# A two-layer hybrid token mixer: order of the transposed attention weights, and recurrence scores in half-width blocks

## The chip, the cores and the metric

The kernel runs on one core of one Trainium2 chip. The metric is the device time of one execution in microseconds; the time before is the median of three runs. TensorE (PE in the profile, its weight loads PEld), VectorE (DVE), ScalarE (ACT), GpSimd (POOL) and SyncE (SP, which issues most DMAs) each work through their own queue in program order and wait for each other by semaphores.

## The reference, cut to what matters

Two layers. Each one normalizes and modulates 512 latent and 256 context tokens of width 1024, mixes them, projects the result, and runs a SwiGLU. The mixer has three parts side by side; the change touches the first two.

```python
# recurrence: 4 heads of width 128, forward and reversed, in chunks
def step(state, inp):
    qi, ki, vi, gi = inp
    bcum = jnp.cumsum(gi, axis=2)
    o_inter = jnp.einsum('bhtk,bhkv->bhtv', qi * jnp.exp(bcum), state)
    rel = bcum[:, :, :, None, :] - bcum[:, :, None, :, :]
    decay = jnp.exp(jnp.where(incl, rel, -jnp.inf))
    scores = jnp.einsum('bhtk,bhsk,bhtsk->bhts', qi, ki, decay)
    o_intra = jnp.einsum('bhts,bhsv->bhtv', scores, vi)
    ...

# differential attention: 4 heads, two maps each
def diff_softmax_attend(q, keys, vals, lam):
    s = jnp.einsum('bqhmd,bkhmd->bhmqk', q, keys).astype(jnp.float32) * (DA_QK ** -0.5)
    p = jax.nn.softmax(s, axis=-1)
    w = p[:, :, 0] - lam * p[:, :, 1]
    return jnp.einsum('bhqk,bkhv->bqhv', w.astype(vals.dtype), vals)
```

Latent queries read 768 keys, context queries (layer 0 alone) the 256 context keys.

## The kernel before

All tokens stay on chip in one SBUF arena, cut into regions that the profile calls reg0 to reg8. PSUM is one tile P of eight banks of 512 columns. The large projections are split into a high and a low part and run as three fp32r matmuls (mm3); the recurrence and the attention's transposes and value products run in plain fp32.

The program is written by a planner. The class Builder holds a model of each engine's time (Clock). A main lane is a generator over the projections (mixer, wout, ffn); side lanes are generators for the recurrence (gla_levels, gla_post), the attention (attention) and others. A side lane yields the model time at which its next step can start; drive takes a main step, then the side steps that are due. So what stands between two steps of a side lane in TensorE's queue is the main lane's work, and the yielded times decide how much. A yield of free(b) is the model's time at which bank b has been read out; written(x) the time at which x is in place.

**Recurrence.** For each head gla_levels computes the scores of all chunks of 128 tokens (six in layer 0, four in layer 1) by seven levels. At level lev blocks of 2^lev tokens meet their neighbours: one matmul per chunk with KM as stationary operand and a strided view of QP as moving operand, into bank 3 or 4 and bank 5 (dst), then a predicated copy through a mask into the score tile. The mask of a level below 6 selects only pairs inside the same 64 tokens; level 6 selects the pairs across the two halves, and is already computed in two 64x64 matmuls per chunk, output partitions 0 to 63 and 64 to 127 in turn. One more group of matmuls, ahead of the loop, computes the diagonal's scores; ScalarE copies it whole. In the trace the levels are P<-reg2f,reg6f and, at level 6, P<-reg2f,reg3f in layer 0; P<-reg0f,reg8f and P<-reg0f,reg1f in layer 1. Each fp32 matmul is two rows.

**Attention.** One unit is a tile of 128 queries and a head: 24 units in layer 0 (16 with 768 keys, 8 with 256), 16 in layer 1. Iteration i of the loop works on four units at once: scores of unit i (two maps, each with a minimum on VectorE and an exponential on ScalarE), transposes of unit i-2 (six tiles, four into bank 4 and two into bank 5), weights of unit i-1 on VectorE, values of unit i-3. The value products vo(u) lie in the upper half of bank 5, so they cannot be written while an engine still reads the transposes in its lower half. transposed(u) copies the transposes out: all 768 columns by ScalarE, or 512 by ScalarE and 256 by VectorE (L280), as the model finds the engines less busy. In the trace the scores are P<-reg2r and P<-reg0r with 96 rows, the transposes P<-reg8f,reg3f and P<-reg8f,reg1f (L246), the values P<-reg6f,reg3f and P<-reg6f,reg1f with 64 columns, the minimum is L956.

Of the kernel before, what the change touches and what calls it, by code (L numbers as in the profile page):

```python
# [19 lines left out]
T = SEQ + CTX  # L20
# [130 lines left out]
class Builder:  # L151
# [580 lines left out]
    def gla_levels(self, h):  # L732
# [23 lines left out]
        def mixed(s):  # L756
            nb0 = (T - t0) // (2 * s)
            self.act(self.V(KM + t0, (2 * s, nb0), (s, 2), (1, s)), self.V(KS + t0, (2 * s, nb0), (s + T, 2), (1, s)))
        yield
        for c in chunks:  # L760
            self.mm(dst(1, c), self.S(self.osc(h, c), 128), self.S(q + c * 128, 128))
        for c, n, b, co in groups(1):
            self.act(self.S(self.osc(h, c), n * 128), self.B(b, n * 128, co))
        mixed(1)
# [2 lines left out]
        for lev in range(7):  # L767
            s = 1 << lev
            nb = T // (2 * s)
            dims = ((2 * s, 64 // s), (s + T, 2), (1, s))  # L770
            for c in chunks:
                if lev == 6:
                    for hf in range(2):
                        o = dst(lev, c, 64 * (1 - hf), 64)
                        self.mm(o[64 * hf:64 * hf + 64], self.S(KS + T * hf + 128 * c + 64 * hf, 64),
                                self.S(QP + T * (1 - hf) + 128 * c + 64 * (1 - hf), 64))
                else:
                    self.mm(dst(lev, c), self.S(KM + 128 * c, 128), self.V(QP + 128 * c, *dims))
            b0 = t0 // (2 * s)
            bd = ((2 * s, nb), (1, s))  # L780
            bl = ((2 * s, nb - b0), (1, s))
# [133 lines left out]
    def attention(self):  # L915
# [58 lines left out]
                self.stt(p0, p1, sm(u, 6), p0, ALU.mult, ALU.add)  # L974

        def transposes(u):
            for k in range(keys(units[u][1])[1]):
                self.tr(self.B(4, 128, k * 128), self.S(pr(u, 0) + k * 128, 128))

        def transposed(u):  # L980
            nk, _ = keys(units[u][1])
            wt = WT + (u % 2) * 768
            if nk < T or self.ck.t['ac'] < self.ck.t['dv']:
                self.act(self.S(wt, nk), self.W(2048, nk))
            else:
                self.act(self.S(wt, 512), self.B(4))
                self.copy(self.S(wt + 512, 256), self.B(5, 256))

        def vo(u):
            return self.B(5, 64, 256 + 64 * (u % 4))  # L990
# [39 lines left out]
        for i in range(n + 3):  # L1030
            if i < n:
                j, t, hh = units[i]
                restack()
                while j and hh not in restacked:
                    yield self.now + 1000
                    restack()
                yield max(self.ck.written(self.S(self.stk(k) + 2 * hh * T, 2 * T)) for k in range(2))
                yield free(0)
                free(0)
                scores(i, 0)  # L1040
            if 0 <= i - 2 < n:
                yield self.ck.written(self.S(pr(i - 2, 0), 256))
                transposes(i - 2)
            if i < n:
                soft(i, 0)
            if 0 <= i - 2 < n:
                transposed(i - 2)
            if 0 <= i - 1 < n:
                weights(i - 1)
            if i < n:  # L1050
                yield free(1)
                free(1)
                scores(i, 1)
                issued = i + 1
            if i >= 3:
                yield self.ck.written(self.S(WT + (i - 3) % 2 * 768, keys(units[i - 3][1])[0]))
                values(i - 3)
            if i < n:
                soft(i, 1)
            if i >= 3:  # L1060
                valued(i - 3)
            finish()
# [401 lines left out]
    def start(self):  # L1464
# [23 lines left out]
            load()  # L1488
        nc.gpsimd.memset(self.S(L.mh, 24), -0.5)
        nc.vector.memset(self.S(L.condT, 256), 0.0)  # L1490
        self.act(self.V(L.condT, (32, 8), (1, 2)), self.V(L.u, (2, 8), (1, 2)), AF.Silu)
        nu = 0

# [203 lines left out]
```

## Time and profile before

| | |
|---|---|
| median of 3 runs | 1910.64 us (1908.35 to 1911.82) |
| profiled execution, its own time | 1918.52 us |
| its span | 1916.7 us |
| busy: TensorE, VectorE, ScalarE, GpSimd | 1833.3, 1038.9, 685.5, 203.1 us |
| mean granted clock of TensorE | 0.985 |

The span is counted from the first to the last instruction of one profiled execution. All positions below are in microseconds from its start. A row of the timeline gives start, duration, engine, line and operation; several equal instructions in a row are merged and counted (x12). A bracket holds how long the engine had been idle before the row and what ended that.

### The profile page before, as it was taken

The page shows a single profiled execution, that of the slowest core. Times are in us where ns is not written, and L with a number is a line of the kernel's source. Part 1 is how long each engine was busy: PE and PEld are TensorE (multiplying, and loading weights), DVE is VectorE, ACT ScalarE, POOL GpSimd, SP SyncE. Part 2 cuts the span into 40 slices and gives each one's busy share as a digit, 9 for nine tenths or more (in the row PEclk, how much of TensorE's full clock was granted, in tenths as well). Part 3 has the DMA queues.
Part 4 walks back from the last instruction along what each step waited for, and adds up shares of the span by engine and source line. Part 5 has one row for each costly group of instructions (what it writes and reads, how often), then busy time and mean ns, then how long its engine had stood idle before and what let it go on. Part 6 is the DMA issues. An engine that isn't in the chain of part 4 may idle for free.

```text
span 1916.7 us, 26273 instructions
## 1 busy us (share of the span) xinstructions
PE 1833.3 (96%) x10580; PEld 1544.2 (81%) x10580; DVE 1038.9 (54%) x1775; ACT 685.5 (36%) x1374; POOL 203.1 (11%) x286
## 2 busy tenths in 40 slices
PE   6999999988899999999999999999988989999998
PEld 3889995577789888888888878889767778888876
DVE  3478753567365666555455374877566442343344
ACT  4533331256463321212212273333256543232222
POOL 0000002233320000000000040000433210000002
PEclk9999999998999999999999999999999989999999
DMA  8211108534042443434343212111422123233321
GB/s 336 67 45 45 34 23 197 152 70 91 1 154 67 144 153 99 154 111 143 110 144 109 67 44 77 45 48 54 87 61 48 53 81 104 72 121 99 98 89 55
DMA packets 52778, 179.82 MB, mean 94 GB/s; under 512 B 6960, under 2 KB 7856, under 8 KB 52656
## 3 DMA queue, kind: packets, MB, share of 16 engines
q1 hardware_dynamic: 48816, 169.48, 27.4%
q0 software_dynamic: 3840, 8.65, 3.4%
q8 instruction: 83, 1.36, 0.3%
q14 instruction: 39, 0.32, 0.1%
HBM read 167.36 MB, written 2.10 MB: 88 GB/s over the span
## 4 chain that ended last, share of the span: by engine, by line
PE 84%; DVE 6%; ACT 5%; DMA 2%; issue 1%; POOL 1%; SPq 0%; DVEq 0%; POOLq 0%; ACTq 0%
PE P L236 82%; PE P L246 3%; DVE reg8f L956 1%; ACT reg1f L257 1%; ACT reg3f L257 1%; DMA reg8f<-in_wmod 1%; ACT reg7r L257 1%; DVE reg7r L264 1%; ACT reg8f L257 1%; DVE reg4f L264 0%; DMA reg4f<-in_wmod 0%; DMA reg0r<-reg5r 0%; POOL reg8f L284 0%; DVE reg8f L276 0%; DVE reg4f L276 0%
## 5 line engine op out<-in xcount | busy, mean ns | idle before, releaser
L236 PE MATMUL P<-reg2r,reg7r 128*128 128x256 f32 (+1 forms) x1920 | 480.7, 338 | 0.2 <-ACT reg8f L257 0.2
L236 PE MATMUL P<-reg0r,reg7r 128*128 128x512 f32 (+1 forms) x1344 | 380.4, 363 | 3.9 <-ACT reg0r L257 3.9
L264 DVE TENSOR_TENSOR reg7r<-reg8f,reg7r 128x1024 fp32r<-128x1024 f32 x201 | 244.7, 1227 | 241.4 <-ACT reg7r L257 239.9
L236 PEld LDWEIGHTS P<-reg2r,reg7r 128*128 128x128 f32 x1920 | 330.1, 190 | 37.8 <-issue 0.7
L257 ACT ACTIVATE reg7r<-reg8f 128x1024 fp32r<-128x1024 f32 x204 | 212.8, 1053 | 370.2 <-issue 150.8
L236 PE MATMUL P<-reg7r,reg0r 128*128 128x512 f32 (+1 forms) x1272 | 329.5, 390 | 6.3 <-ACT reg0r L257 5.9
L236 PE MATMUL P<-reg3r,reg7r 128*128 128x512 f32 (+1 forms) x960 | 321.5, 335 | 0.4 <-DVE reg3r L264 0.4
L236 PEld LDWEIGHTS P<-reg0r,reg7r 128*128 128x128 f32 x1344 | 243.4, 191 | 51.1 <-issue 8.8
L236 PEld LDWEIGHTS P<-reg7r,reg0r 128*128 128x128 f32 x1272 | 233.1, 190 | 56.7 <-ACT reg0r L257 6.8
L236 PE MATMUL P<-reg1r,reg7r 128*128 128x512 f32 (+1 forms) x672 | 241.4, 359 | 0.6 <-DVE reg1r L264 0.6
L236 PE MATMUL P<-reg7r,reg2r 128*128 128x512 f32 (+1 forms) x912 | 234.1, 385 | 3.4 <-ACT reg2r L257 1.5
L236 PEld LDWEIGHTS P<-reg3r,reg7r 128*128 128x128 f32 x960 | 182.3, 190 | 18.5 <-issue 0.7
L236 PEld LDWEIGHTS P<-reg7r,reg2r 128*128 128x128 f32 x912 | 167.0, 190 | 37.1 <-ACT reg2r L257 2.3
L236 PEld LDWEIGHTS P<-reg1r,reg7r 128*128 128x128 f32 x672 | 128.7, 191 | 18.7 <-DVE reg1r L264 1.1
L276 DVE SCALAR_TENSOR_TENSOR reg8f<-reg8f 128x512 f32<-128x512 f32 (+3 forms) x154 | 88.5, 574 | 10.8 <-DMA reg8f<-in_wmod 7.9
L236 PE MATMUL P<-reg7r,reg1r 128*128 128x512 f32 (+1 forms) x240 | 90.9, 379 | 0.1
L956 DVE TENSOR_REDUCE reg8f<-P 128x1 f32<-128x768 f32 (+1 forms) x80 | 67.5, 845 | 42.5 <-PE P L236 41.4
L257 ACT ACTIVATE reg3f<-P,reg8f 128x768 f32<-128x768 f32 (+3 forms) x96 | 52.6, 570 | 85.2 <-DVE reg8f L956 64.4
L284 POOL TENSOR_TENSOR reg8f<-reg8f 128x1 f32<-128x1 f32 (+2 forms) x102 | 60.6, 595 | 184.8 <-ACT reg5f L257 100.9
L236 PE MATMUL P<-reg7r,reg3r 128*128 128x512 f32 (+1 forms) x192 | 70.9, 369 | 0.0
L257 ACT ACTIVATE reg0r<-reg1f 128x256 fp32r<-128x256 f32 (+1 forms) x46 | 23.5, 511 | 132.4 <-DVE reg1f L264 132.4
L264 DVE TENSOR_TENSOR reg5f<-reg5f,P 128x512 f32<-128x512 f32 x60 | 40.8, 685 | 47.3 <-PE P L236 47.2
(217 smaller groups left out, 2083.3 us busy)
## 6 DMA issues: line engine op xcount, KB each, us to landing
reg8f<-in_wfi SPq DMA_DIRECT2D x88, 512.0 KB, 3.6
reg8f<-in_wmod SPq DMA_DIRECT2D x80, 512.0 KB, 3.6
reg8f<-in_win SPq DMA_DIRECT2D x56, 512.0 KB, 3.5
reg8f<-in_wfo SPq DMA_DIRECT2D x44, 512.0 KB, 3.6
reg8f<-in_wout SPq DMA_DIRECT2D x16, 512.0 KB, 3.6
reg6f<-in_xin SPq DMA_DIRECT2D x12, 512.0 KB, 7.0
reg2r<-reg5r POOLq DMA_DIRECT2D x24, 192.0 KB, 7.2
reg2f<-in_wmod SPq DMA_DIRECT2D x8, 512.0 KB, 6.2
```

The costliest lines, as they stand in the source:

```text
L236: self.nc.tensor.matmul(out, lhsT, rhs, start=start, stop=stop)
L246: self.nc.tensor.transpose(out, in_, self.S(self.L.ident, 128))
L257: self.nc.scalar.activation(out=out, in_=in_, func=func, **kw)
L264: self.nc.vector.tensor_tensor(out=out, in0=a, in1=b, op=op)
L276: self.nc.vector.scalar_tensor_tensor(out=out, in0=a, scalar=s, in1=b, op0=op0, op1=op1)
L284: self.nc.gpsimd.tensor_tensor(out=out, in0=a, in1=b, op=op)
L956: self.nc.vector.tensor_reduce(out=sm(i, 2 + m), in_=x, axis=AX.X, op=ALU.min)
```

## The change

1. Recurrence, the group ahead of the loop and levels 0 to 5: one 128x128 matmul per chunk becomes two of 64x64 on the diagonal, written to output partitions 0 to 63 and 64 to 127 in turn. The off-diagonal blocks are no longer written; a memset of banks 3 to 5 at the start gives them a defined content.
2. Attention, unit with six key tiles: the two transposes into bank 5 come first; VectorE always copies them out, in the same step; ScalarE copies the other 512 columns, ahead of the exponential of the unit that is being scored.
3. Attention, yields: the transposes now wait in the model for banks 4 and 5 as well, the values for bank 5.

```diff
         for c in chunks:
-            self.mm(dst(1, c), self.S(self.osc(h, c), 128), self.S(q + c * 128, 128))
+            for hf in (0, 64):
+                self.mm(dst(1, c, hf, 64)[hf:hf + 64], self.S(self.osc(h, c) + hf, 64), self.S(q + c * 128 + hf, 64))
...
-            dims = ((2 * s, 64 // s), (s + T, 2), (1, s))
+            dims = ((2 * s, 32 // s), (s + T, 2), (1, s))
...
-                    self.mm(dst(lev, c), self.S(KM + 128 * c, 128), self.V(QP + 128 * c, *dims))
+                    for hf in (0, 64):
+                        self.mm(dst(lev, c, hf, 64)[hf:hf + 64], self.S(KM + 128 * c + hf, 64), self.V(QP + 128 * c + hf, *dims))
...
         def transposes(u):
-            for k in range(keys(units[u][1])[1]):
+
+            nk, kt = keys(units[u][1])
+            wt = WT + (u % 2) * 768
+            for k in (4, 5, 0, 1, 2, 3) if kt == 6 else range(kt):
                 self.tr(self.B(4, 128, k * 128), self.S(pr(u, 0) + k * 128, 128))
-
-        def transposed(u):
-            nk, _ = keys(units[u][1])
-            wt = WT + (u % 2) * 768
-            if nk < T or self.ck.t['ac'] < self.ck.t['dv']:
-                self.act(self.S(wt, nk), self.W(2048, nk))
-            else:
-                self.act(self.S(wt, 512), self.B(4))
+            if kt == 6:
                 self.copy(self.S(wt + 512, 256), self.B(5, 256))
+            self.act(self.S(wt, min(nk, 512)), self.W(2048, min(nk, 512)))
...
-                yield self.ck.written(self.S(pr(i - 2, 0), 256))
+                yield max(self.ck.written(self.S(pr(i - 2, 0), 256)), self.ck.free(4), self.ck.free(5))
                 transposes(i - 2)
             if i < n:
                 soft(i, 0)
-            if 0 <= i - 2 < n:
-                transposed(i - 2)
...
-                yield self.ck.written(self.S(WT + (i - 3) % 2 * 768, keys(units[i - 3][1])[0]))
+                yield max(self.ck.written(self.S(WT + (i - 3) % 2 * 768, keys(units[i - 3][1])[0])), self.ck.free(5))
                 values(i - 3)
...
+        nc.vector.memset(self.W(3 * 512, 3 * 512), 0.0)
```

TensorE's queue in layer 1, middle of the attention, before. L246 are transposes, reg0r the scores, 64x64 the values, reg7r and reg8f with 256 columns the main lane's work:

```order
L236 MATMUL P<-reg6f,reg1f 64x64 x12
L236 MATMUL P<-reg8f,reg4f 128x256 x2
L236 MATMUL P<-reg0r 128x512
L236 MATMUL P<-reg0r 128x256
L236 MATMUL P<-reg8f,reg4f 128x256 x2
L246 MATMUL P<-reg8f,reg1f 128x128 x6
L236 MATMUL P<-reg0r 128x512
L236 MATMUL P<-reg0r 128x256
L236 MATMUL P<-reg6f,reg1f 64x64 x12
```

The same stretch of TensorE's queue after:

```order
L236 MATMUL P<-reg6f,reg1f 64x64 x12
L236 MATMUL P<-reg0r 128x512
L236 MATMUL P<-reg0r 128x256
L236 MATMUL P<-reg8f,reg4f 128x256 x2
L246 MATMUL P<-reg8f,reg1f 128x128 x6
L236 MATMUL P<-reg0r 128x512
L236 MATMUL P<-reg0r 128x256
L236 MATMUL P<-reg8f,reg4f 128x256 x2
L236 MATMUL P<-reg6f,reg1f 64x64 x12
```

Main work has moved from behind the values to in front of them. In the last seven units of this stage none is left; TensorE's queue after, there:

```order
L236 MATMUL P<-reg6f,reg1f 64x64 x12
L236 MATMUL P<-reg0r 128x512
L236 MATMUL P<-reg0r 128x256
L246 MATMUL P<-reg8f,reg1f 128x128 x6
L236 MATMUL P<-reg0r 128x512
L236 MATMUL P<-reg0r 128x256
L236 MATMUL P<-reg6f,reg1f 64x64 x12
```

Before, each of those units but the last ones held two to ten matmuls of the main lane. ScalarE's queue in layer 1, two units before (768 columns from P and reg8f is an exponential, 512 or 768 columns from P the copy of transposes, 64 columns the scaled values):

```order
L257 ACTIVATE reg1f,reg8f<-P,reg8f 128x768
L257 ACTIVATE reg1f<-P 128x512
L257 ACTIVATE reg1f,reg8f<-P,reg8f 128x768
L257 ACTIVATE reg1f<-P,reg8f 128x64
L257 ACTIVATE reg8f<-reg1f 128x64
L257 ACTIVATE reg7r<-reg8f 128x1024
L257 ACTIVATE reg8f<-P 128x512
L257 ACTIVATE reg1f,reg8f<-P,reg8f 128x768
L257 ACTIVATE reg1f<-P 128x768
L257 ACTIVATE reg1f,reg8f<-P,reg8f 128x768
```

And after:

```order
L257 ACTIVATE reg1f<-P 128x512
L257 ACTIVATE reg1f,reg8f<-P,reg8f 128x768
L257 ACTIVATE reg1f<-P 128x512
L257 ACTIVATE reg1f,reg8f<-P,reg8f 128x768
L257 ACTIVATE reg1f<-P,reg8f 128x64
L257 ACTIVATE reg8f<-reg1f 128x64
L257 ACTIVATE reg8f<-P 128x512 x2
L257 ACTIVATE reg1f<-P 128x512
L257 ACTIVATE reg1f,reg8f<-P,reg8f 128x768 x2
```

The copy stands ahead of the first exponential, and the 768-column form is gone. In the recurrence the two orders differ at the head of a head's work only in the form of the group; both stand between the same rows of the main lane.

## Rows read from the trace of the kernel before

**Rows 1.** Stages: length, busy (x) of PE PEld DVE ACT POOL, clock, DMA

```profile
109.00:281.00 172.00, 170.46 (x1272) 158.26 (x1271) 127.61 (x268) 61.73 (x134) 5.13 (x6) 1.00 0.11 35
...
375.00:503.00 128.00, 110.46 (x870) 88.75 (x869) 75.59 (x158) 76.89 (x212) 46.64 (x46) 0.95 0.31 69
...
1196.00:1332.00 136.00, 136.00 (x965) 124.29 (x964) 107.29 (x230) 49.97 (x108) 4.66 (x6) 1.00 0.14 44
...
1386.00:1490.00 104.00, 85.66 (x684) 72.04 (x685) 64.61 (x123) 58.41 (x141) 34.89 (x34) 0.93 0.25 50
```

**Rows 2.** TensorE's waits in both attention stages: releaser, us in total, times, longest

```profile
PE P L236 <- DVE reg3f L280: 8.0, 7, 2.3
PE P L236 <- ACT reg3f L257: 6.1, 4, 2.4
...
PE P L236 <- DVE reg1f L280: 9.5, 11, 2.4
PE P L236 <- ACT reg1f L257: 7.1, 3, 4.0
```

**Rows 3.** Timeline of TensorE, layer 0, first head: levels 0, 1, 5 and 6

```profile
112.76 2.16 PE L236 MATMUL P<-reg2f,reg6f 128*128 128x128 f32 x12
114.62 0.54 PE L236 MATMUL P<-reg0r,reg7r 128*128 128x512 f32 x1
...
118.86 1.60 PE L236 MATMUL P<-reg2f,reg6f 128*128 128x128 f32 x12
120.21 0.38 PE L236 MATMUL P<-reg0r,reg7r 128*128 128x256 f32 x1
...
133.65 0.28 PE L236 MATMUL P<-reg0r,reg7r 128*128 128x256 f32 x1
133.77 1.50 PE L236 MATMUL P<-reg2f,reg6f 128*128 128x128 f32 x12
135.03 0.36 PE L236 MATMUL P<-reg0r,reg7r 128*128 128x256 f32 x1
...
137.14 0.28 PE L236 MATMUL P<-reg0r,reg7r 128*128 128x256 f32 x1
137.35 0.92 PE L236 MATMUL P<-reg2f,reg3f 128*64 128x64 f32 x24
138.20 0.50 PE L236 MATMUL P<-reg0r,reg7r 128*128 128x512 f32 x1
```

**Rows 4.** Timeline of TensorE, layer 1, first head: levels 5 and 6

```profile
1218.91 1.06 PE L236 MATMUL P<-reg0f,reg8f 128*128 128x128 f32 x8
1219.72 0.47 PE L236 MATMUL P<-reg2r,reg7r 128*128 128x512 f32 x1
...
1224.02 0.69 PE L236 MATMUL P<-reg0f,reg1f 128*64 128x64 f32 x16
1224.63 0.50 PE L236 MATMUL P<-reg2r,reg7r 128*128 128x512 f32 x1
```

**Rows 5.** Timeline around the longest wait of the values, layer 1

```profile
1423.28 0.80 ACT L257 ACTIVATE reg1f<-P 128x768 f32<-128x768 f32 x1
...
1424.13 2.46 PE L236 MATMUL P<-reg6f,reg1f 128*64 128x64 f32 x24 [3.96 <-ACT reg1f L257]
```

**Rows 6.** Timeline of a quiet unit of layer 1, several engines

```profile
1450.23 0.90 ACT L257 ACTIVATE reg1f<-P,reg8f 128x768 f32<-128x768 f32 x1 [0.84 <-DVE reg8f L956]
...
1451.13 0.31 ACT L257 ACTIVATE reg1f<-P,reg8f 128x64 f32<-128x64 f32 x1
...
1451.96 0.82 PE L246 MATMUL P<-reg8f,reg1f 128*128 128x128 f32 x6
...
1452.53 0.59 PE L236 MATMUL P<-reg0r 96*128 96x512 f32 x2
...
1452.88 0.42 DVE L280 COPY reg1f<-P 128x256 f32<-128x256 f32 x1 [0.56 <-PE P L246]
...
1453.36 1.43 PE L236 MATMUL P<-reg6f,reg1f 128*64 128x64 f32 x24 [0.24 <-DVE reg1f L280]
...
1454.72 1.13 PE L236 MATMUL P<-reg8f 128*128 128x256 f32 x4
...
1455.19 0.90 ACT L257 ACTIVATE reg1f<-P,reg8f 128x768 f32<-128x768 f32 x1 [0.85 <-DVE reg8f L956]
```

## The prediction, made before the changed kernel ran

> **What bounds the kernel now.** I read the busy time by stage first [rows 1]; the reader is to look for stages in which TensorE's column falls short of the stage's length. In the recurrence stages (109 to 281 us in layer 0, 1196 to 1332 us in layer 1) TensorE has work for 170.46 of 172 us and for all of 136 us: there every nanosecond that a matmul gives back is a nanosecond of the span, so long as VectorE (127.61 of 172, 107.29 of 136) keeps up. The two attention stages (375 to 503 and 1386 to 1490 us) are the only long ones where it does not run through: busy 110.46 of 128 and 85.66 of 104, so 17.5 + 18.3 = 35.9 us idle, at a mean granted clock of 0.95 and 0.93. TensorE's waits in these two, longest first, say for what [rows 2]: 8.0 + 9.5 us for the DVE copy of transposed weights (L280) and 6.1 + 7.1 us for ScalarE, mostly its form of the same copy. Together 30.7 of the 35.9 us. The edit has one part in either kind of stage.
>
> **Part 1, half-width recurrence scores.** Seven groups per head (the score before the loop, then levels 0 to 5) change from one 128x128 to two 64x64 blocks per chunk: 6 full matmuls become 12 half ones in layer 0, 4 become 8 in layer 1. In the trace each of these fp32 matmuls is two instructions, so a full group of layer 0 reads x12 and a half one x24. The order puts the half groups in the same places, 12 in a row. The loop's level 6 already has exactly the new form: full contraction, 64 columns, alternating output halves. So its price is in the trace. I take starts, since the ends are modelled. A full layer-0 group takes 133.77 to 135.03, 1.26 us; level 6 takes 137.35 to 138.20, 0.85 us, and begins 0.21 us after the matmul ahead where the full group begins 0.12 us after one of the same width, so 0.09 us more on entry: 0.94 us [rows 3]. That saves 0.32 us a group. In layer 1 a full group takes 0.81 us, level 6 0.61 us and, with the same entry, 0.70 us: 0.11 us a group [rows 4].
>
> Two levels are not like that. At level 0 the moving operand is read element by element from two places, and the full group takes 1.86 us instead of 1.26 [rows 3]. If two strided streams cannot be read side by side, halving the columns gains nothing and the entry costs 0.09 us; if they can, the group falls to 0.94 us. The extra 0.60 us looks like reading, not arithmetic, so I take no gain, and keep both ends. Level 1 (runs of two) takes 1.35 us [rows 3]; it may keep that, or fall to 0.94; I take 1.0 us, since it lies near the plain 1.26. Sum per head in layer 0: five plain groups 5 x 0.32 = 1.60, level 1 0.35, level 0 -0.09: 1.86 us, by four heads 7.4 us. In layer 1: 5 x 0.11 + 0.11 - 0.09 = 0.57, by four 2.3 us. Part 1 gives **9.7 us**; with no gain at level 1 it is 7, with level 0 gaining all of the way from 1.95 to 0.94 in layer 0, 1.0 us a head, and two thirds of that in layer 1, where a group is four matmuls, it is 16.
>
> Entering and leaving the narrow form is what speaks against this part. The Trainium skill, "TensorEngine Tiling (Array Packing)", section Key Properties, says that changing the tiling mode drains TensorE. The trace shows a drain of 0.09 us on entry at level 6, and no figure stands on the page; by the rule alone 56 groups would lose 56 x 0.09 = 5 us, by the rows that is inside the 0.94 and 0.70 us above and the group still comes out cheaper.
>
> A memset of 1536 PSUM columns joins VectorE's queue at the start, behind the one of 128x256. VectorE has nothing else to do there until the first modulation is reduced, and no bank it writes is used by that first product. I cost it at nothing; without that cover it would be under 2 us.
>
> **Part 2, attention.** PSUM bank 5 holds the last two transposed weight tiles of one unit and the value products of the unit before. So the values wait until that bank has been copied out. What the edit moves: the two transposes into bank 5 go first of six; VectorE always copies that bank (before, the planner gave all 768 columns to ScalarE for six of the 32 units with six key tiles); ScalarE's 512-column copy goes ahead of the exponential; and the planner, which did not know of the wait, now holds the values until the bank is free and puts main work in front.
>
> The worst wait shows what goes: the values at 1424.13 had waited 3.96 us for the 768-column copy at 1423.28, which stood behind an exponential that had to wait for its own minimum [rows 5]. With VectorE the copy stands behind the minimum only. Six such waits shrink to the VectorE kind. In a quiet unit the VectorE kind costs 0.24 us [rows 6]: the copy at 1452.88 starts when the last transpose is through; two transposes first instead of last frees it 4 x 0.11 = 0.44 us sooner, unless the minimum is later.
>
> What is late next: main work is not made, only moved. The order of the new kernel puts 0.9 to 2.8 us of it before transposes and values in the first units and has none left for four whole units in layer 0 and five in layer 1, near the end of each stage. An uncovered unit is set by a loop through three engines: exponential, scaling of the values on ScalarE (frees bank 5), transposes, VectorE copy, weights, minimum, next exponential. In the quiet unit that loop runs from 1450.23 to 1455.19, 4.96 us [rows 6], with about 0.2 us of main work in its way. The new transposes' order takes 0.44 us from it: 4.3 us as an estimate, 4.96 as the other end. TensorE's own work in a unit, by starts, is transposes 0.57, two scores at most 0.59 each, values 1.36: 3.1 us [rows 6]. So an uncovered unit leaves 1.2 to 1.9 us idle, nine of them 11 to 17 us; I take 13, nearer the lower end because the loop stands there in full [rows 6]. The other 31 units I give 0.2 us each, after the 0.24 us of the quiet one [rows 6]: 6 us; 0 to 0.6 us each are the ends (0 to 19). 5 us of the old idle time had other causes and stays; 4 us I keep for copies that still stand behind a weight split on VectorE. Sum 28 us against 35.9: **8 us**. Ends: 11 + 0 + 5 gives 20 us gain, 17 + 19 + 5 gives 5 us loss.
>
> ScalarE's copy now delays the exponential by its 0.59 us. Behind it wait the sums for the weights and the next unit's scores on the same bank; in the loop above the exponential of the second map is released by VectorE's minimum, so the first has about that much room. It is part of the worse end.
>
> **How the numbers follow.** The profiled execution took 1918.5 us (span 1916.7), 7.9 us over the median of 1910.6. 1918.5 - 9.7 - 8 = 1900.8 us; less 7.9 that is **1893 us**. Both ends together: 16 + 20 gives 1875, 7 - 5 gives 1909. This kernel's runs tell about 0.2% (3.8 us) from no change.
>
> **Rivals.**
> 1. Attention is a wash: the idle time moves from the value waits to the uncovered units, as the sum 41 of 35.9 at its worse end allows. Then only part 1 counts: 1910.6 - 9.7 = 1901 us. For it: main work is the same in sum. Against: the old waits of 2 to 4 us were longer than any loop needs.
> 2. Slower, by the clock: nine uncovered units in a row run at half clock. The values after the 3.96 us wait took 2.46 us, the usual 1.43 [rows 5, 6]: a pause was followed by the low level. At 1.2 GHz the 3.1 us of a unit are 6.2, with the unit's 1.2 us of waiting 7.4 instead of 4.3: 9 x 3.1 = 28 us, 1921 us. It decides from seven of the nine units on (7 x 3.1 = 21.7 us, the 17.7 gained and 0.2%). Against: the uncovered pauses should be 1 to 2 us each, half of the 3.96 us one or less [rows 5]. The Trainium skill, "TensorE: Matmul & The Clock Gate", section HAM oscillation, warns of such pauses between bursts; the clock of these two stages, 0.95 and 0.93, agrees that it happens here.
> 3. The halves do not overlap when both read all partitions: then a half instruction costs what one of the values costs, 1.36 us for 24, 57 ns [rows 6]. A group takes 1.36 + 0.09 = 1.45 us, 0.19 more than 1.26, and in layer 1 also 0.19 more: 56 x 0.19 = 10.6 us lost in place of 9.7 gained, 1913 us. Level 6 at 35 ns an instruction speaks against it.
> 4. VectorE, 74% and 79% busy in the recurrence [rows 1], sets the pace of the levels and part 1's gain is given back as waiting: 1902.6 us. Against: it has 44 and 29 us to spare there, and TensorE hardly waits.
>
> Chances: forecast 0.46, rival 1 0.22, rival 4 0.09, rival 2 0.11, rival 3 0.08, and 0.04 for a little of everything that ends within 0.2%. Faster by more than 0.2%: 0.77; within 0.2%: 0.12; slower: 0.11. The range 1879 to 1909 takes in the forecast's ends but for their joint extreme, and rivals 1 and 4; rivals 2 and 3 lie outside.
>
> **What would show it.** Right: plain half groups of layer 0 start-to-start at 0.85 us, of layer 1 at 0.61; TensorE's wait for L280 and for ScalarE in the attention stages under half of 30.7 us; uncovered units of 4.3 to 5 us with the pause in front of the transposes. Wrong: half groups of 1.4 us (rival 3); level 0 well below 1.86 (part 1 too small); a granted clock under 0.9 late in either attention stage (rival 2); TensorE pauses at the recurrence groups, released by VectorE (rival 4).

## The result, and the profile after

| | before | after |
|---|---|---|
| median, and lowest to highest | 1909.49 us (1907.67 to 1911.82) | 1882.89 us (1880.88 to 1886.66) |
| profiled execution, its span | 1918.52, 1916.7 us | 1883.15, 1881.0 us |
| TensorE busy | 1833.3 us | 1812.2 us |
| span less TensorE busy | 83.4 us | 68.8 us |
| mean granted clock | 0.985 | 0.991 |

The changed kernel is 26.6 us faster: 0.9856 of the time before (95%: 0.9843 to 0.9869). The forecast was 1893 us, the range 1879 to 1909. The head of the page after, with the busy times of all engines:

```profile
span 1881.0 us, 27410 instructions
PE 1812.2 (96%) x11140; PEld 1507.5 (80%) x11140; DVE 1040.1 (55%) x1781; ACT 684.0 (36%) x1374; POOL 208.1 (11%) x287
```

The span fell by 35.7 us: 21.1 us of TensorE's busy time and 14.6 us of its idle time. Of that idle time 3.4 us need not be the edit's: between the recurrence and the attention of layer 0 the profiled run of before waited 5.5 us for transfers of in_wmod, the changed kernel 2.1; and the run y0 below, whose matmuls are those of before one by one up to there, waited 0.8. VectorE and ScalarE are busy for as long as before. The busy time by stage, in windows that answer to [rows 1] (the stages now begin and end sooner):

```profile
109.00:268.00 159.00, 157.90 (x1590) 138.95 (x1589) 127.06 (x268) 61.65 (x134) 7.42 (x6) 1.00 0.13 38
360.00:486.00 126.00, 113.30 (x883) 87.82 (x882) 77.79 (x165) 76.15 (x213) 47.47 (x46) 0.96 0.32 72
1177.00:1312.00 135.00, 134.42 (x1204) 115.30 (x1203) 107.80 (x231) 51.13 (x109) 3.66 (x6) 1.00 0.15 44
1362.00:1457.00 95.00, 83.64 (x703) 69.33 (x703) 67.53 (x127) 58.76 (x144) 38.91 (x36) 0.98 0.29 60
```

The recurrence of layer 0 does VectorE's same 127 us of work in 159 us instead of 172, and TensorE still runs through. In the two attention stages TensorE is idle for 12.7 and 11.4 us, 24.1 in place of 35.9, and their clock rose from 0.95 and 0.93 to 0.96 and 0.98. TensorE's timeline in layer 0, first head, for [rows 3]: levels 0, 1, 5 and 6, each with the row behind it:

```profile
112.67 1.22 PE L236 MATMUL P<-reg2f,reg6f 128*64 128x64 f32 x24
113.82 0.50 PE L236 MATMUL P<-reg0r,reg7r 128*128 128x512 f32 x1
...
118.13 0.96 PE L236 MATMUL P<-reg2f,reg6f 128*64 128x64 f32 x24
119.03 0.39 PE L236 MATMUL P<-reg0r,reg7r 128*128 128x256 f32 x1
...
132.38 0.92 PE L236 MATMUL P<-reg2f,reg6f 128*64 128x64 f32 x24
133.23 0.39 PE L236 MATMUL P<-reg0r,reg7r 128*128 128x256 f32 x1
...
135.79 0.92 PE L236 MATMUL P<-reg2f,reg3f 128*64 128x64 f32 x24 [0.87 <-DVE reg6f L793]
136.64 0.50 PE L236 MATMUL P<-reg0r,reg7r 128*128 128x512 f32 x1
```

Start to start, level 0 takes 1.15 us (before 1.86), level 1 0.90 (1.35), a plain level 0.85 (1.26), and level 6, which was not changed, 0.85. The same in layer 1, levels 0 and 5, for [rows 4]:

```profile
1181.01 0.88 PE L236 MATMUL P<-reg0f,reg8f 128*64 128x64 f32 x16
1181.82 0.50 PE L236 MATMUL P<-reg2r,reg7r 128*128 128x512 f32 x1
...
1199.13 0.69 PE L236 MATMUL P<-reg0f,reg8f 128*64 128x64 f32 x16
1199.75 0.50 PE L236 MATMUL P<-reg2r,reg7r 128*128 128x512 f32 x1
```

0.81 us (before 1.19 to 1.32) and 0.62 (0.81). What TensorE waits for in the two attention stages, first layer 0 and then layer 1, for [rows 2]; L246 are the transposes, L236 scores and values:

```profile
PE P L246 <- ACT reg3f L257: 6.9, 7, 1.6
PE P L236 <- ACT reg3f L257: 2.6, 3, 1.5
...
PE P L246 <- ACT reg1f L257: 7.5, 7, 1.6
...
PE P L236 <- ACT reg1f L257: 0.9, 1, 0.9
```

VectorE's copy (L280), 17.5 us before, is gone from the list; the values and scores wait 3.5 us for ScalarE instead of 13.2. In their place stands one new wait, 14 times about 1 us in front of the transposes. One whole unit without main work, several engines, from one exponential of the second map to the next (answers to [rows 6]):

```profile
1432.82 0.90 ACT L257 ACTIVATE reg1f<-P,reg8f 128x768 f32<-128x768 f32 x1 [0.46 <-DVE reg8f L959]
...
1433.71 0.30 ACT L257 ACTIVATE reg1f<-P,reg8f 128x64 f32<-128x64 f32 x1
...
1434.15 0.85 PE L246 MATMUL P<-reg8f,reg1f 128*128 128x128 f32 x6 [1.07 <-ACT reg1f L257]
...
1434.67 0.43 DVE L280 COPY reg1f<-P 128x256 f32<-128x256 f32 x1 [0.52 <-PE P L246]
...
1435.28 1.43 PE L236 MATMUL P<-reg6f,reg1f 128*64 128x64 f32 x24
...
1435.99 0.95 DVE L959 TENSOR_REDUCE reg8f<-P 128x1 f32<-128x768 f32 x1
...
1436.98 0.90 ACT L257 ACTIVATE reg1f<-P,reg8f 128x768 f32<-128x768 f32 x1 [0.46 <-DVE reg8f L959]
```

The loop of the prediction stands there link by link: exponential, scaled values (bank 5 free), transposes, VectorE's copy, its three small steps for the weights (1435.01 to 1436.08, not shown), minimum, exponential: 1432.82 to 1436.98, 4.16 us, of which TensorE waits 1.07.

Two stretches made of such units, columns as in [rows 1]:

```profile
451.00:467.00 16.00, 11.96 (x135) 9.85 (x135) 12.18 (x25) 11.15 (x33) 7.94 (x7) 1.00 0.00 1
1421.00:1448.00 27.00, 19.80 (x220) 16.14 (x219) 19.64 (x40) 19.71 (x53) 11.80 (x9) 1.00 0.01 1
```

TensorE waits there about 1.1 us in every 4.2, and its granted clock stays at 1.00, the level of 2.4 GHz.

### The profile page after: what moved, and what is told of

Read it like the earlier page. It is cut to its first block, busy times and chain, and to the rows that moved or that the text cites. A ratio compares the mean times of both kernels' runs of the same rounds, so it can differ in the third digit from the quotient of the medians.

```text
span 1881.0 us, 27410 instructions
## 1 busy us (share of the span) xinstructions
PE 1812.2 (96%) x11140; PEld 1507.5 (80%) x11140; DVE 1040.1 (55%) x1781; ACT 684.0 (36%) x1374; POOL 208.1 (11%) x287
## 3 DMA queue, kind: packets, MB, share of 16 engines
q8 instruction: 87, 1.43, 0.3%
## 4 chain that ended last, share of the span: by engine, by line
PE 85%; DVE 5%; ACT 5%; DMA 2%; issue 1%; POOL 1%; SPq 0%; DVEq 0%; POOLq 0%; ACTq 0%
PE P L236 82%; PE P L246 3%; ACT reg1f L257 1%; ACT reg3f L257 1%; DVE reg8f L959 1%; ACT reg7r L257 1%; DVE reg7r L264 1%; ACT reg8f L257 1%; DMA reg4f<-in_wmod 0%; DMA reg8f<-in_wmod 0%; DMA reg0r<-reg5r 0%; DVE reg4f L264 0%; DMA reg8f<-in_wout 0%; ACT reg0r L257 0%; DVE reg8f L276 0%
## 5 line engine op out<-in xcount | busy, mean ns | idle before, releaser
L236 PE MATMUL P<-reg2r,reg7r 128*128 128x256 f32 (+1 forms) x1920 | 481.0, 338 | 0.2 <-ACT reg8f L257 0.2
L236 PE MATMUL P<-reg0r,reg7r 128*128 128x512 f32 (+1 forms) x1344 | 380.3, 363 | 3.9 <-ACT reg0r L257 3.9
L236 PEld LDWEIGHTS P<-reg2r,reg7r 128*128 128x128 f32 x1920 | 330.2, 190 | 39.1 <-issue 0.7
L236 PE MATMUL P<-reg7r,reg0r 128*128 128x512 f32 (+1 forms) x1272 | 328.5, 389 | 8.1 <-ACT reg0r L257 6.1
L236 PE MATMUL P<-reg3r,reg7r 128*128 128x512 f32 (+1 forms) x960 | 321.9, 335 | 0.4 <-DVE reg3r L264 0.4
L236 PEld LDWEIGHTS P<-reg0r,reg7r 128*128 128x128 f32 x1344 | 243.1, 191 | 52.5 <-issue 8.4
L236 PEld LDWEIGHTS P<-reg7r,reg0r 128*128 128x128 f32 x1272 | 233.2, 190 | 58.0 <-ACT reg0r L257 7.1
L236 PE MATMUL P<-reg1r,reg7r 128*128 128x512 f32 (+1 forms) x672 | 241.3, 359 | 0.6 <-DVE reg1r L264 0.6
L236 PE MATMUL P<-reg7r,reg2r 128*128 128x512 f32 (+1 forms) x912 | 231.4, 382 | 5.6 <-DVE reg3r L276 1.9
L236 PEld LDWEIGHTS P<-reg7r,reg2r 128*128 128x128 f32 x912 | 165.7, 188 | 39.4 <-ACT reg2r L257 2.3
L236 PEld LDWEIGHTS P<-reg3r,reg7r 128*128 128x128 f32 x960 | 182.4, 190 | 18.5 <-issue 0.7
L236 PEld LDWEIGHTS P<-reg1r,reg7r 128*128 128x128 f32 x672 | 128.3, 191 | 18.7 <-DVE reg1r L264 1.1
L236 PE MATMUL P<-reg7r,reg1r 128*128 128x512 f32 (+1 forms) x240 | 90.6, 378 | 0.1
L284 POOL TENSOR_TENSOR reg8f<-reg8f 128x1 f32<-128x1 f32 (+2 forms) x102 | 60.2, 592 | 182.5 <-ACT reg5f L257 98.5
L236 PE MATMUL P<-reg7r,reg3r 128*128 128x512 f32 (+1 forms) x192 | 70.0, 364 | 0.0
L257 ACT ACTIVATE reg3f<-P 128x512 f32<-128x512 f32 (+2 forms) x106 | 45.1, 442 | 65.5 <-PE P L246 34.7
```

The source lines that it names most:

```text
L236: self.nc.tensor.matmul(out, lhsT, rhs, start=start, stop=stop)
L257: self.nc.scalar.activation(out=out, in_=in_, func=func, **kw)
L284: self.nc.gpsimd.tensor_tensor(out=out, in0=a, in1=b, op=op)
```

## The experiments

**How to read the times.** Each run lists its mean granted clock beside its time. The time that a run loses to the clock is at most (1 - clock) x span: all of it if TensorE had work throughout, less where it was idle. For the kernel before that is 22 us of 1912. Taking it off also takes off most of the spread: in the second group of runs the seven times of before differ by 2.8 us (standard deviation), without that loss by 0.8; in the third 2.8 and 1.1, in the first (15 runs) 3.0 and 2.3. So in two of the three groups the spread of the times of before is mostly its clock. Over the 89 runs of all kernels, 1 us more of that loss than the kernel's mean goes with 0.78 us more of time: taking all of it off takes off somewhat too much. All results, with the mean of this loss and of what is left ("the rest"); kernels of one group ran on one chip beside the kernel before:

| kernel | median us | ratio (95%) | clock loss | the rest |
|---|---|---|---|---|
| before, groups 1 to 3 | 1912.1, 1910.4, 1912.3 | | 22.0, 21.8, 23.2 | 1889.6, 1889.6, 1888.8 |
| changed kernel | 1882.89 | 0.9856 (0.9843, 0.9869) | 16.0 | 1867.3 |
| 1: p1, scores alone | 1907.05 | 0.9967 (0.9951, 0.9983) | 27.2 | 1878.7 |
| 1: p2, attention alone | 1894.53 | 0.9915 (0.9892, 0.9937) | 16.6 | 1878.1 |
| 1: na, halves not in turn | 1903.11 | 0.9960 (0.9944, 0.9976) | 17.1 | 1885.8 |
| 1: va, values in turn | 1880.20 | 0.9839 (0.9816, 0.9862) | 25.8 | 1854.3 |
| 2: ny, no new yields | 1889.96 | 0.9887 (0.9865, 0.9908) | 21.7 | 1868.2 |
| 2: to, old transposes' order | 1880.19 | 0.9841 (0.9815, 0.9867) | 15.5 | 1865.8 |
| 2: ea, copy after exponential | 1881.72 | 0.9846 (0.9825, 0.9868) | 18.8 | 1863.5 |
| 2: oc, old choice of engine | 1879.15 | 0.9836 (0.9810, 0.9862) | 16.9 | 1862.6 |
| 3: yo, scores and yields | 1885.17 | 0.9862 (0.9839, 0.9884) | 19.3 | 1866.3 |
| 3: y0, yields alone | 1893.34 | 0.9913 (0.9884, 0.9942) | 15.1 | 1879.0 |
| 3: d1300, yields 1300 ns early | 1888.75 | 0.9879 (0.9859, 0.9899) | 23.6 | 1865.2 |
| 3: vd, d1300 and va | 1880.57 | 0.9834 (0.9812, 0.9855) | 26.3 | 1853.9 |

The clock is given to three digits, so a single run's loss is known to 1 us. The theory at the outset: the scores save what their groups save (15 us, 63.4 to 48.4 by starts over all 56, entry included), and the attention edit saves the waits of the values. The rival: what one part frees is given back elsewhere.

### The two parts apart: p1 and p2

p1 is the changed kernel with the attention as before:

```diff
-                yield max(self.ck.written(self.S(pr(i - 2, 0), 256)), self.ck.free(4), self.ck.free(5))
+                yield self.ck.written(self.S(pr(i - 2, 0), 256))
```

and likewise the yield of the values, the transposes' order and transposed(u) as before.

> The half-width scores alone, attention as before. Theory A (the two parts act apart and add): the starts of the score groups in the two traces differ by 15.0 us in sum (63.4 us before, 48.4 after, entry of 0.09 us counted), TensorE is the bound there, so 1909.5 - 15 = 1894.5 us. Rival B (part of that comes back as waiting later, and the attention has given most): 1900 us or more.

Measured 1907.05 us, 0.33% faster (0.17 to 0.49). The first theory falls: of the 15 us about 5 are left (5.1 by the medians, 5.7 by the means). The busy times on p1's page:

```profile
PE 1824.6 (95%) x11140; PEld 1519.9 (80%) x11140; DVE 1040.0 (54%) x1778; ACT 684.2 (36%) x1374; POOL 204.1 (11%) x285
```

TensorE's waits in p1's attention stage of layer 0:

```profile
PE P L236 <- DVE reg3f L280: 11.3, 10, 3.4
PE P L246 <- ACT reg3f L257: 4.5, 5, 1.4
PE P L236 <- ACT reg3f L257: 2.9, 2, 2.3
```

Both attention stages with the work just ahead of them, by busy time, columns as in [rows 1]; two rows of before, then two of p1:

```profile
335.00:503.00 168.00, 149.60 (x1054) 113.07 (x1053) 97.22 (x202) 86.99 (x232) 55.22 (x52) 0.96 0.37 90
1372.00:1491.00 119.00, 99.19 (x751) 82.38 (x750) 73.52 (x135) 63.15 (x150) 42.27 (x39) 0.94 0.25 53
...
323.00:494.00 171.00, 149.35 (x1035) 111.01 (x1035) 99.33 (x203) 84.92 (x230) 54.01 (x51) 0.95 0.35 86
1367.00:1485.00 118.00, 98.25 (x749) 81.72 (x748) 73.01 (x134) 63.06 (x150) 41.70 (x39) 0.94 0.26 53
```

Layer 0's values wait 11.3 us for L280 where [rows 2] have 8.0, and the stage's 171 us hold 21.7 us without TensorE work where before's 168 hold 18.4; in layer 1 both have 19.8. The span, 1910.7, less busy is 86.1 us of idle time, 2.7 more than before, and the clock's loss in the table is 5.2 us higher than before's. Without that loss p1 is 10.9 us faster than before, where the means give 5.7. So half of what is missing is TensorE's clock, and a part the longer waits.

That lower clock is only in part in the attention. In the profiled runs the granted clock from 20 to 60 us is 0.87 in p1 and 0.91 before, though TensorE's queues are the same up to 109 us; from 300 to 330 us, ahead of layer 0's attention, 0.89 and 0.94; then the rows above, 0.95 and 0.96 in layer 0, 0.94 in both in layer 1. Each of the first three is worth 1.5 to 1.8 us, and the first at least lies ahead of every changed matmul.

p2 is the attention part alone, the scores as before:

```diff
-            for hf in (0, 64):
-                self.mm(dst(1, c, hf, 64)[hf:hf + 64], self.S(self.osc(h, c) + hf, 64), self.S(q + c * 128 + hf, 64))
+            self.mm(dst(1, c), self.S(self.osc(h, c), 128), self.S(q + c * 128, 128))
```

and likewise levels 0 to 5, without the memset.

> The attention part alone, score groups 128 wide as before. Theory A: the rest of the gain, 1909.5 - 11.6 = 1898 us, with uncovered units of 4.2 us. Rival B: 1890 us or less.

Measured 1894.53 us, 17.6 faster than before: between the two expectations. The page:

```profile
PE 1822.3 (96%) x10580; PEld 1532.2 (81%) x10580; DVE 1040.2 (55%) x1781; ACT 683.9 (36%) x1374; POOL 205.0 (11%) x287
```

The span is 1889.5, so 67.2 us idle, 16.2 fewer; and TensorE is busy 11.0 us less with as many instructions as before, at a granted clock of 0.993 in this profile where before's has 0.985. In the table: 11.5 us in the rest, 5.4 in the clock. **The two parts add up in the rest:** 10.9 + 11.5 = 22.4 us, the changed kernel 22.1 (1867.3 against before's mean of 1889.4). In the times they give 5.1 and 17.6 alone, 22.7, and 26.6 together. The clock's column has the missing 3.9 us, since p1 loses 5 us more to the clock than before and the changed kernel 6 us less; but the intervals (3 us to either side for p1, 4 for p2, 2.5 for the changed kernel) would allow such a gap by themselves. That the times do not add is not shown.

### Why half groups are cheap: na

na writes all chunks' halves of one side before those of the other (levels 0 to 5; the lines that wrote them in turn go):

```diff
+            for hf, c in [(hf, c) for hf in (0, 64) for c in chunks if lev < 6]:
+                self.mm(dst(lev, c, hf, 64)[hf:hf + 64], self.S(KM + 128 * c + hf, 64), self.V(QP + 128 * c + hf, *dims))
```

> The changed kernel, but in levels 0 to 5 all upper halves are issued first and then all lower ones, so that neighbours use the same half. Theory A (a half is cheap because its neighbour in the other half runs beside it): a plain group of layer 0 goes from 0.85 us to 24 x 57 ns = 1.37, of layer 1 from 0.62 to 0.91, 24 groups each, 12 + 7 = 19 us slower than the changed kernel, about 1902 us. Rival B (a 64-column matmul is cheap by itself): 1883 us as the changed kernel.

Measured 1903.11 us, as the first theory had it, and the rest is 18.4 us above the changed kernel's. Levels 0 and 2 of the first head:

```profile
111.18 1.92 PE L236 MATMUL P<-reg2f,reg6f 128*64 128x64 f32 x24
113.03 0.50 PE L236 MATMUL P<-reg0r,reg7r 128*128 128x512 f32 x1
...
121.08 1.43 PE L236 MATMUL P<-reg2f,reg6f 128*64 128x64 f32 x24
122.44 0.38 PE L236 MATMUL P<-reg0r,reg7r 128*128 128x256 f32 x1
```

A plain group takes 1.36 us, 57 ns an instruction, in place of 0.85 and 35 ns: rival 3's price exactly, and dearer than the full group of 1.26. Level 0 takes 1.85 in place of 1.15. So the gain of part 1 is not that half of the columns are dropped; it is that neighbours in the queue write opposite halves and run side by side, strided reading included. The starts of single instructions at level 0 show it: na starts one every 84 ns (111.30, 111.38 us), the changed kernel two, 7 ns apart, every 84 ns (112.79, 112.87). The Trainium skill, "TensorEngine Tiling (Array Packing)", section Key Properties, says that different tiles operate independently and may run in parallel; these two rows, 57 and 35 ns, agree.

### The same for the values: va and vd

```diff
-            for hf in (0, 64):
-                for k in range(kt):
+            for k in range(kt):
+                for hf in (0, 64):
```

> The changed kernel with one thing more: the value products alternate their halves tile by tile instead of finishing one half first. Theory A (neighbours in different halves run side by side): 24 instructions take 0.85 us instead of 1.36; in the 23 covered units with six key tiles that is on TensorE's path, 23 x 0.5 = 11 us, in the uncovered ones the loop hides it: about 1871 us. Rival B (accumulating halves in one bank can't run side by side, or all units are set by the loop): 1881 to 1885 us.

Measured 1880.20 us. TensorE in one uncovered unit of layer 1:

```profile
1429.85 0.84 PE L246 MATMUL P<-reg8f,reg1f 128*128 128x128 f32 x6 [1.13 <-ACT reg1f L257]
1430.45 0.59 PE L236 MATMUL P<-reg0r 96*128 96x512 f32 x2
1430.97 0.92 PE L236 MATMUL P<-reg6f,reg1f 128*64 128x64 f32 x24
1432.27 0.62 PE L236 MATMUL P<-reg0r 96*128 96x512 f32 x2 [0.38 <-ACT reg1f L257]
1434.01 0.85 PE L246 MATMUL P<-reg8f,reg1f 128*128 128x128 f32 x6 [1.13 <-ACT reg1f L257]
```

The values take 0.92 us instead of 1.43 (in 18 units with work behind them 0.85 us by starts, instead of 1.36), and the unit still 4.16 (1429.85 to 1434.01): the loop of the other engines sets it. Elsewhere the gain is there, 13 us in the rest, so the halves do run side by side; but the clock loses 9.8 us more than in the changed kernel, and 2.7 us of median remain, within the intervals. The time is near the rival's (1881 to 1885), though the halves do run side by side. vd is va with both new yields 1300 ns earlier.

> The same earlier yields and the value products alternating their halves. Theory A (with main work in every unit the 0.5 us per value group is on TensorE's path): 1864 to 1871 us. Rival B (the units are set by their loop of 4.2 us, the halves only add idle time and low clock): 1877 to 1884 us.

1880.57 us, the rival's: the rest is 1853.9, the lowest of all with va's, and the clock loss, 26.3, is one of the two highest. Starting the attention's steps earlier does not get the gain out.

### What in the attention edit matters: ny, y0, yo, to, ea, oc, d1300

ny takes the two yields back and keeps the orders and copies:

```diff
-                yield max(self.ck.written(self.S(pr(i - 2, 0), 256)), self.ck.free(4), self.ck.free(5))
+                yield self.ck.written(self.S(pr(i - 2, 0), 256))
...
-                yield max(self.ck.written(self.S(WT + (i - 3) % 2 * 768, keys(units[i - 3][1])[0])), self.ck.free(5))
+                yield self.ck.written(self.S(WT + (i - 3) % 2 * 768, keys(units[i - 3][1])[0]))
```

> The changed kernel with the two yields of the attention as before: the planner no longer knows that transposes and values wait for banks 4 and 5; instructions and queues otherwise as changed. Theory A (main work in front of the values is what removed the waits): the values wait again 0.2 to 2 us in the 23 covered units, the tail's nine units get main work back: 1890 to 1896 us, TensorE's wait for L280 over 15 us. Rival B (who copies the bank, and when, removed the waits): 1881 to 1886 us.

1889.96 us, 7 slower than the changed kernel, at the near end of the first theory. Its waits for the copy, from the list of all waits of TensorE:

```profile
PE P L236 <- DVE reg1f L280: 13.2, 8, 4.3
...
PE P L236 <- DVE reg3f L280: 8.0, 5, 2.9
```

21.2 us of waits for L280 are back, more than the 17.5 of before. Yet the rest is only 0.9 us above the changed kernel's: the larger part of what it loses, 5.7 us, is in the clock. y0 is the opposite, the kernel before with the two yields and nothing else (the two + lines of the edit in the section on the change).

> The kernel before with the two new yields and nothing else, score groups 128 wide. Theory A: as the attention part alone, 1892 to 1898 us. Rival B: 1903 us or more.

1893.34 us against p2's 1894.53: the yields alone do all that the attention part does. yo puts the half-width scores beside them.

> Half-width scores and the two new yields of the attention, nothing else: transposes in the old order, the old rule of who copies, ScalarE's copy behind the exponential. Theory A (the yields alone remove the value waits; the rest of the attention edit is worth nothing measurable): 1879 to 1886 us, as the changed kernel. Rival B (they need VectorE's early copy): 1888 us or more, with waits of the values for ScalarE over 8 us.

1885.17 us, 0.9862 against the changed kernel's 0.9856. So with the yields in, the orders and copies are not worth anything that these runs can tell. Without the yields they are: from p1 to ny, where they are the only difference, the ratio falls from 0.9967 to 0.9887. Each of the two suffices to take 10 to 12 us off the rest (p1's 1878.7 to 1868.2 and 1866.3), and they do not add (1867.3 with both). The single pieces, each undone in the changed kernel, agree. The transposes in the old order:

```diff
-            for k in (4, 5, 0, 1, 2, 3) if kt == 6 else range(kt):
+            for k in range(kt):
```

> The changed kernel with the six transposes in their old order, bank 5 last. Theory A (the loop of an uncovered unit runs through transposes and VectorE's copy): that loop is 4 x 0.11 = 0.44 us longer, uncovered units 4.2 to 4.6 us, nine of them 4 us: 1887 us. Rival B (ScalarE's queue sets the loop): uncovered units stay at 4.2, 1883 us.

1880.19 us. TensorE in an uncovered unit of it:

```profile
1429.95 0.87 PE L246 MATMUL P<-reg8f,reg1f 128*128 128x128 f32 x6 [0.95 <-POOL reg1f L284]
...
1431.41 1.43 PE L236 MATMUL P<-reg6f,reg1f 128*64 128x64 f32 x24 [0.24 <-DVE reg1f L280]
...
1434.35 0.87 PE L246 MATMUL P<-reg8f,reg1f 128*128 128x128 f32 x6 [0.96 <-POOL reg1f L284]
```

The unit takes 4.40 us, 0.24 more than with bank 5 first, and what releases its transposes is another: GpSimd's sum of the weights (L284). Nine units of 0.24 us are 2 us, under what the runs tell. ScalarE's copy behind the exponential:

```diff
+            if 0 <= i - 2 < n:
+                copied(i - 2)
```

where copied(u) holds the self.act that stood at the end of transposes(u).

> The changed kernel with ScalarE's copy behind the first exponential, as before. Theory A (VectorE's copy alone frees the bank that the values wait for): 1881 to 1885 us. Rival B (ScalarE's place ahead of the exponential matters for the next unit): more than 1886 us, with waits of TensorE released by ScalarE.

1881.72 us, no difference. The planner's old choice, all 768 columns by ScalarE where it is less busy:

```diff
-            if kt == 6:
+            if kt == 6 and self.ck.t['ac'] >= self.ck.t['dv']:
                 self.copy(self.S(wt + 512, 256), self.B(5, 256))
-            self.act(self.S(wt, min(nk, 512)), self.W(2048, min(nk, 512)))
+                nk = 512
+            self.act(self.S(wt, nk), self.W(2048, nk))
```

> The changed kernel with the old rule of who copies: ScalarE all 768 columns where the planner finds it less busy, which is now most of the units with six key tiles. Theory A (ScalarE's copy was slow because it stood behind an exponential; ahead of it it is only 0.8 against 0.41 us and waits for all six transposes): values wait some 0.5 us more in uncovered units, VectorE is relieved by as much: 1883 to 1888 us. Rival B (VectorE's copy is what counts): 1890 us or more.

1879.15 us, below both expectations, with 21 units copied by ScalarE. In an uncovered unit TensorE shows:

```profile
1427.91 1.43 PE L236 MATMUL P<-reg6f,reg1f 128*64 128x64 f32 x24 [0.56 <-ACT reg1f L257]
1429.28 0.61 PE L236 MATMUL P<-reg0r 96*128 96x512 f32 x2
1429.97 0.85 PE L246 MATMUL P<-reg8f,reg1f 128*128 128x128 f32 x6
1430.58 0.59 PE L236 MATMUL P<-reg0r 96*128 96x512 f32 x2
1431.72 1.43 PE L236 MATMUL P<-reg6f,reg1f 128*64 128x64 f32 x24 [0.56 <-ACT reg1f L257]
```

3.81 us a unit (1427.91 to 1431.72) in place of 4.16: with the copy off VectorE the loop is shorter. The copy that the edit always gives to VectorE lies in the very loop that sets these units. The median is 3.7 us below the changed kernel's, within the intervals. d1300 subtracts 1300 from both yields:

```diff
-                yield max(self.ck.written(self.S(pr(i - 2, 0), 256)), self.ck.free(4), self.ck.free(5))
+                yield max(self.ck.written(self.S(pr(i - 2, 0), 256)), self.ck.free(4), self.ck.free(5)) - 1300
```

> The changed kernel with both new yields 1300 ns earlier, so that less main work stands in front of each and nearly every whole unit keeps some. Theory A (the uncovered units' 1.1 us of idle time, nine times, can be covered): 1873 to 1878 us. Rival B (with less work in front the values wait again, as much as the tail saves): 1881 to 1888 us.

1888.75 us, just above the rival's 1881 to 1888: with the steps due earlier the values wait for L280 again (10.8 us in its list of waits), and again the rest stays, 1865.2, and the clock loss rises, 23.6.

## Why the prediction was right, and where it was off

**The side and the range: right, the sum in part by luck.** 1882.89 lies in 1879 to 1909, but 10 us under the forecast. Alone, the parts gave 5.1 and 17.6 us of time where 9.7 and 8 were forecast: one miss covers a piece of the other. In the profiled pair three causes come to most of the difference: 15.0 us of score groups, 11.8 us of idle time in the attention stages, and the clock there. Before it lost 128 x 0.05 + 104 x 0.07 = 13.7 us at most, after 126 x 0.04 + 95 x 0.02 = 6.9: 6.8. Together 33.6 of 35.7 us; but the last two overlap, since a stretch at low clock is counted whole, waits included, and the 3.4 us of waiting for in_wmod are outside of all three. The pair differs by more than the medians because the profiled run of before, 8 us over its median, had a clock of 0.985 where before's runs average 0.9885, 6.7 us, and had those waits. Taking that run's surplus off, as the prediction did, was right. Its worse end was not the worst: the 4 us kept for copies are in the forecast and not in the ends, with them it is 1913 us.

**Part 1, the plain groups: right.** 0.85 us and 0.62, and the entry of 0.09 us that level 6 had shown: a half group of layer 0 begins 0.32 us behind a 512-column matmul where the full group began 0.23 us behind it. VectorE (rival 4) is out: TensorE's whole idle time in the recurrence of layer 0 is 1.1 us, 0.87 of it the wait at 135.79. The memset that was put at nothing takes VectorE 1.34 us from 1.44 us on, and the first changed group starts at 109.53 us where before's started at 109.32. Rival 3 is out, and na shows that its price was right for halves that are not in turn.

**Part 1, level 0: the term that was mis-sized.** "No gain at level 0" was chosen because its extra 0.60 us looked like reading. It is reading, and two strided reads do run side by side: 1.15 us, with its entry 1.24, in place of the 1.95 allowed. Level 1 came to 0.99 with its entry, as taken. Over all groups 15.0 us came out where 9.7 was taken, close to the end of 16 that the prediction kept, and level 0 is most of that miss.

**Part 1 counted as net: wrong in p1, hidden in the sum.** "There every nanosecond that a matmul gives back is a nanosecond of the span" holds for the stage, not for the kernel: alone, part 1 brought 5 us of time. In p1's profile the attention of layer 0 waits 3 us longer, and the granted clock is lower there and, not by the edit, at the start. The rule on drains of the Trainium skill, "TensorEngine Tiling (Array Packing)", section Key Properties, did not decide: the 56 entries are inside the 15.0 us.

**Part 2, the loop: right.** The pause stands in front of the transposes, the units take 4.2 us (forecast 4.3) and leave 1.1 us idle (forecast 1.2 to 1.9), four in layer 0 and five in layer 1 as the order showed. Two numbers under it were off: the transposes' order is worth 0.24 us of the loop, not 0.44, and the mark "ScalarE and L280 under half of 30.7 us" was badly set, since the pause in front of the transposes is itself a wait for ScalarE: 17.9 us in total, though only 3.5 of the old kind.

**Part 2, the sum: 8 us forecast, 11.8 us of idle time measured, and a gain of clock that the sum left out.** The nine uncovered units leave about 10 us (13 taken), all other waits of the two stages 14 (15 taken). The larger miss is the clock. The prediction had it as a loss only (rival 2), and held the low clock of 0.95 and 0.93 constant in the forecast itself. The values' long pauses went, and half of those stages' loss with them; that the one brought the other is not shown. Rival 1 (a wash) is out by p2. Rival 2 is out by the two stretches of uncovered units, at 1.00 throughout. The low level came at other places: from 426 to 442 us, ahead of layer 0's uncovered units, the granted clock is 0.68, with waits of 1.60 and 1.61 us in that stretch and one of 1.45 just before it.

**Part 2, which edit: wrong.** The prediction let the copy's engine and the transposes' order do the work and the yields only move main work. y0 and yo show that the yields alone are enough. ny shows that the orders and copies alone bring nearly as much of the rest (1868.2, from p1's 1878.7) and end 7 us behind in time; and oc shows that VectorE's copy, one of them, lengthens the loop.

**What stays open.** Why the clock's loss is higher in p1, va, vd, ny and d1300 than in the changed kernel. In the profiles of p1 and va a part of it lies at the start, where nothing that TensorE does was changed (0.87 from 20 to 60 us, 0.91 in the changed kernel). In all five TensorE pauses in the attention stages in other places or for longer than in the changed kernel, or does the work between two pauses in less time; no run changed the pauses and nothing else. The clock loss is an upper bound, since the time that TensorE idles at the low clock is counted in it. Of the 15.0 us of p1's groups, 10.9 are in the rest; 2.7 us of the difference is idle time, the remainder is within what the clock's loss is known to.

## What to carry to other kernels

Here two half-width matmuls in place of a full one paid when neighbours in the queue wrote opposite halves, and cost when they did not (0.85 and 1.36 us a group, 1.26 for the full one): look at the order before the column count. Where a planner orders the work, telling it of a wait (a bank that must be free) can be worth as much as shortening that wait, and the two need not add: here either took 10 to 12 us off the rest, and both together no more. Add up a change's clock as well as its busy and idle time: read the granted clock of each stage, and compare kernels with the clock's loss taken off before asking why two gains don't add.

## What the runs showed of the hardware that was not expected

- Two strided fp32 reads on opposite output halves run side by side: 48 ns an instruction at level 0 (1.15 us for 24), on the same half 77 ns (1.85), full width 155 ns (1.86 for 12).
- Value products in turn take 35 ns each (0.85 us for 24, by starts, in va) where one half after the other takes 57 (1.36).
- Units in which TensorE waits about 1.1 us in every 4.2 us ran at a granted clock of 1.00 throughout (451 to 467 and 1421 to 1448 us of the changed kernel).
- Most of the spread of the times of before is the granted clock in two groups of seven runs: 2.8 us of standard deviation become 0.8 to 1.1 with its loss taken off. In the group of fifteen 3.0 become 2.3.
- A kernel with 13 us less in the rest (va) ended only 3 us faster; its granted clock was 0.986 on average where the changed kernel's was 0.9915.
